# Hybrid decoder layer on one core: loads, closings, pacing and the weighting of the carried keys are changed

## The chip, the cores and the metric

The kernel runs on one core of a Trainium2 chip. The core has five engines: TensorE (PE in the profile; its weight loads are PEld), VectorE (DVE), ScalarE (ACT), GpSimd (POOL) and SyncE (SP), which here issues the DMA transfers. The metric is the device time of one execution in microseconds; lower is better. Kernels are compared by the medians of several executions.

## The reference

One decoder layer on x of 1024 tokens x 1024 features in fp32, with a memory of 256 tokens:

```
h   = rmsnorm(x, ln1);  z = h @ w_in            # mLSTM q,k,v,o,gates; forgetting q,k,v,gates
ml  = mlstm_chunkwise(silu(conv(q)), silu(conv(k)) * dh**-0.5, v, i, log_sigmoid(f))   # 4 heads of 128
        # carried along:  C = decay*C + sum_s wa_s v_s k_s ;  n = decay*n + sum_s wa_s k_s
        # num = scores @ v + inter * C q ;  den = sum(scores) + inter * n.q ;  out = num / max(|den|, exp(-m))
fx  = softmax(q k^T * dh**-0.5 + c_t - c_s, causal) @ v      # 8 heads of 64, c = cumsum(log_sigmoid(f))
x  += concat(norm(ml) * sigmoid(o), fx) @ w_out
x  += cross_attention(rmsnorm(x, ln_x), rmsnorm(mem, ln_mem))  # 4 heads of 256
x  += relu(rmsnorm(x, ln2) @ w_ff1)**2 @ w_ff2               # 1024 -> 4096 -> 1024
out = rmsnorm(x, ln_f)
```

## The kernel before

**Numbers.** A product in fp32 is made of three matmuls with operands split in a high and a low half (`mm3`, L184: low x high, high x low, high x high; these are L186, L187 and L188 in the profile). `split` (L131) makes the halves: ScalarE copies the high half (L134, or L137 with a scale), VectorE subtracts to get the low one (L135, or L138).

**Tiles.** Working tiles come from tagged slots: `w2` is 128x512 with a letter (`r_a` to `r_y` in the profile), `z` tiles are 128x1024 and a little more, `w` and `act` are larger. A tile waits until the tile that had its slot before is done with. PSUM has banks of 128x512 with tags `mm`, `m2` (or `m`), `tp`, `sc`, `ov`. Weights come into `wr` (two tiles of 128x1024) and are cut into `wh` and `wl` (three each).

**What sets the order.** The Python code issues the instructions in a program order; a scheduler with a simulated time then orders them on each engine, by what it takes to be ready first. Only inside `in_order` (L144), which the forgetting stage uses for each slot, does an engine keep the order of the code. All transfers go through SP's queue, in the order there; a transfer whose tile is not free holds those behind it.

**Stages.** First come norms, memory, values and gates; then the four mLSTM heads with the projections of the next head and of the forgetting heads' queries and keys (to about 365 us of the profiled execution); the forgetting heads' scores and values, beside them the filler (to about 605); the rest of the out projection (`w_out_b`), cross-attention and its out projection (to about 860); the MLP's first product, called Up here (to about 1200); its second, Down.

**mLSTM.** Time is cut in two halves of 512. `ml_project` (L657) makes a head's activated keys: `conv_silu` (L500) multiplies, convolves and ends with VectorE's L513 (y = (tanh + 1) * y, feature-major, 128 features x 1024 tokens). `fx_project` does a forgetting projection in between, and then `carried` (L517) makes the state that the first half leaves to the second: it loads the row's maximum, ScalarE makes four columns of weights from the gates (L522), TensorE transposes the first half of the keys (L527), VectorE multiplies the transposed keys by the weights (L529) and the result is split (L536). TensorE then forms the matrix (L540) and, with four matmuls against a column of ones (L542), the vector n_. `carry` (L554) uses both. `ml_head` (L569) does the scores of a head in a generator, whose closing part is stepped through by the next head's `ml_project`.

**Forgetting heads.** `slot` (L1026) does one step of several pipelines at once: transposes of one block of probabilities (`Values.turn`, L779), the product of an earlier one (`add`, L798), maxima (L741, L744), the split of the transposed block (`cut`), ScalarE's exponential (L756, into probabilities, from the bank of `sc` that a `score` of an earlier slot filled), GpSimd's scaling (L760), the next `score` (L728; matmuls L734, L735). When a half of a head has had its last product, `fx_close` (L805) copies the upper half of its `ov` bank with ScalarE (L810) and VectorE adds the lower (L811); the slot after that does no product. `sc` has three uses in flight at most, so a score waits for the exponential of an earlier part.

The filler (L1007) is work that the attention does not need: `key_unit`, `value_unit` (cross-attention's keys and values from the memory) and 16 `out_unit`s (out projection of the part that is there already, weights `w_out_a`). Each is a generator of steps of three matmuls, and each step says what it costs: 1.5 for keys and values, 3.0 for out. A slot n takes steps until the sum of the costs has reached (n − 3) x 4.6 (`RATE`, `DELAY`) or a unit ends. `cut_next` cuts at most one or two half weight tiles per slot (ScalarE L988; VectorE and GpSimd L989) once they are three slots old, and then the next load is issued. What is left of the filler runs behind the last slot without a slot's order (L1108).

**Up.** The product with `w_ff1` is done in blocks of 2 x 2 with seven products instead of eight. `todo` has 16 pairs of weight tiles; `left_up` (L1242) loads a pair (`raw_pair`, L1232: SP, tiles `wr` for odd pairs, two `z` tiles for even ones) and makes the left operands in three groups: group 0 splits the first tile and the half x22 of the second, and forms the sums x21 + x22 (L1256), and from it three further ones (L1257 to L1260; `sub` is L1223), on GpSimd for pairs 2 to 15. `prepare` calls it five jobs ahead of the first job that needs the group; a job is one of the seven products, 12 matmuls. VectorE and GpSimd also form sums of the results, and SP stores them (`put_right`, L1426).

## Time and profile before

| | |
|---|---|
| median of 3 executions | 1522.53 us (1520.9 to 1523.7) |
| profiled execution | 1523.35 us, span of its instructions 1521.6 us |
| mean granted TensorE clock | 0.998 |
| TensorE busy | 1502.7 us, 99% of the span |
| VectorE, ScalarE, GpSimd busy | 1100.3, 727.7, 510.1 us |
| DMA | 299.86 MB, 197 GB/s on the mean |

The profiled execution is 0.8 us above the median. In the profile, a row of a timeline has the start, the length, the engine, the line, the operation, what it writes and reads, shapes, and in brackets how long the engine stood idle before it and what ended the wait. The chain that ended last goes over TensorE for 93% of the span.

### The profile page before, as it was taken

To read this page: it belongs to the slowest core of one execution; us is meant where nothing else is said; L and a number is where in the kernel's file an instruction comes from. 1 tells how busy PE (TensorE), PEld (TensorE's weight loads), DVE (VectorE), ACT (ScalarE), POOL (GpSimd) and SP (SyncE) were. 2 spreads that over 40 slices of the span, in tenths; PEclk is the share of its full clock that TensorE was granted. 3 is DMA by queue.
4 is the path that set the end of the run, shared out by engine and by line. 5 is a ranking of instruction groups with operands and counts; after the bars stand their busy time and mean duration, and the time that the engine had idled before them with its cause. 6 is when DMAs were issued, how large, how long until landed. Compare 5 with 4: busy or idle time off the path is not lost.

```text
span 1521.6 us, 21977 instructions
## 1 busy us (share of the span) xinstructions
PE 1502.7 (99%) x7694; PEld 1261.5 (83%) x7694; DVE 1100.3 (72%) x1743; ACT 727.7 (48%) x1360; POOL 510.1 (34%) x543
## 2 busy tenths in 40 slices
PE   9999999999999999999999999999999999999997
PEld 9988888889999788888888877778787888888887
DVE  7766676765787786944457989898887667787665
ACT  7324343334687665644443456666664621122124
POOL 1003030413364442511110034544555265663322
PEclk9999999999999999999999999999999999999999
DMA  6322223435888886843344437776678777776623
GB/s 239 109 77 87 98 100 114 135 126 157 246 244 267 260 264 230 300 131 124 119 147 157 153 134 277 247 256 242 222 252 286 291 277 276 276 270 248 239 94 111
DMA packets 122538, 299.86 MB, mean 197 GB/s; under 512 B 13614, under 2 KB 28264, under 8 KB 115516
## 3 DMA queue, kind: packets, MB, share of 16 engines
q1 hardware_dynamic: 122428, 298.46, 57.4%
q8 instruction: 60, 0.98, 0.3%
q14 instruction: 50, 0.41, 0.1%
HBM read 199.60 MB, written 98.81 MB: 196 GB/s over the span
## 4 chain that ended last, share of the span: by engine, by line
PE 93%; DVE 3%; ACT 2%; DMA 1%; issue 1%; SPq 0%; DVEq 0%; POOLq 0%; POOL 0%; ACTq 0%
PE tp L186 8%; PE tp L187 8%; PE tp L188 8%; PE m L186 6%; PE sc L186 6%; PE m L187 6%; PE m L188 6%; PE sc L187 6%; PE sc L188 6%; PE mm L186 6%; PE mm L187 6%; PE mm L188 6%; PE ov L186 2%; PE ov L187 2%; PE ov L188 2%; PE ov L801 2%
## 5 line engine op out<-in xcount | busy, mean ns | idle before, releaser
L186 PE MATMUL tp<-act,wl 128*128 128x512 f32 (+1 forms) x440 | 172.9, 393 | 1.2 <-ACT row L1396 0.7
L187 PE MATMUL tp<-act,wh 128*128 128x512 f32 (+1 forms) x440 | 172.1, 391 | 0.0
L188 PE MATMUL tp<-act,wh 128*128 128x512 f32 (+1 forms) x440 | 171.7, 391 | 0.0
L135 DVE TENSOR_TENSOR wl<-wr,wh 128x1024 fp32r<-128x1024 f32 (+2 forms) x95 | 124.5, 1311 | 22.0 <-ACT wh L134 21.4
L134 ACT ACTIVATE wh<-wr 128x1024 fp32r<-128x1024 f32 (+2 forms) x95 | 95.6, 1007 | 75.9 <-PE tp L188 34.7
L186 PE MATMUL mm<-act,wl 128*128 128x512 f32 (+1 forms) x332 | 127.5, 384 | 0.0
L188 PE MATMUL mm<-act,wh 128*128 128x512 f32 (+1 forms) x332 | 127.3, 383 | 0.0
L187 PE MATMUL mm<-act,wh 128*128 128x512 f32 (+1 forms) x332 | 127.2, 383 | 0.0
L186 PE MATMUL m<-act,wl 128*128 128x512 f32 (+1 forms) x308 | 117.7, 382 | 0.5 <-DVE wl L135 0.5
L188 PE MATMUL m<-act,wh 128*128 128x512 f32 (+1 forms) x308 | 117.7, 382 | 0.0
L187 PE MATMUL m<-act,wh 128*128 128x512 f32 (+1 forms) x308 | 117.5, 381 | 0.0
L186 PEld LDWEIGHTS tp<-act,wl 128*128 128x128 f32 x440 | 82.6, 188 | 20.6 <-ACT row L1396 1.2
L188 PEld LDWEIGHTS tp<-act,wh 128*128 128x128 f32 x440 | 82.6, 188 | 18.9
L187 PEld LDWEIGHTS tp<-act,wh 128*128 128x128 f32 x440 | 82.7, 188 | 18.5
L186 PE MATMUL sc<-act,wl 128*128 128x512 f32 (+1 forms) x248 | 97.0, 391 | 1.0 <-DVE wl L135 1.0
L188 PE MATMUL sc<-act,wh 128*128 128x512 f32 (+1 forms) x248 | 96.7, 390 | 0.0
L187 PE MATMUL sc<-act,wh 128*128 128x512 f32 (+1 forms) x248 | 96.6, 390 | 0.0
L1467 POOL TENSOR_TENSOR z<-wr 128x256 f32<-128x256 f32 x56 | 51.7, 944 | 130.6 <-DMA wr<-w_ff2q 116.8
L134 ACT ACTIVATE wh<-z 128x1024 fp32r<-128x1024 f32 (+1 forms) x54 | 55.5, 1028 | 80.8 <-POOL z L1467 58.4
L135 DVE TENSOR_TENSOR wl<-z,wh 128x1024 fp32r<-128x1024 f32 (+1 forms) x54 | 74.3, 1376 | 7.8 <-ACT wh L134 7.6
L134 ACT ACTIVATE w<-wr 128x768 fp32r<-128x768 f32 (+2 forms) x31 | 25.5, 823 | 106.2 <-PE tp L186 33.7
L188 PEld LDWEIGHTS mm<-act,wh 128*128 128x128 f32 x332 | 62.3, 188 | 12.7
(726 smaller groups left out, 4288.4 us busy)
## 6 DMA issues: line engine op xcount, KB each, us to landing
act<-right SPq DMA_DIRECT2D x49, 1024.0 KB
right<-w SPq DMA_DIRECT2D x56, 256.0 KB
wr<-w_ff2q SPq DMA_DIRECT2D x28, 512.0 KB
right<-r_d SPq DMA_DIRECT2D x49, 256.0 KB
right<-r_e SPq DMA_DIRECT2D x49, 256.0 KB
act<-fqk SPq DMA_DIRECT2D x48, 256.0 KB
wr<-w_in SPq DMA_DIRECT2D x20, 512.0 KB
wr<-w_ff SPq DMA_DIRECT2D x20, 512.0 KB
```

The costliest lines, as they stand in the source:

```text
L134: s.activation(hi, src, AF.Copy)
L135: return v.tensor_tensor(out=lo, in0=src, in1=hi.bitcast(F32), op=ALU.subtract)
L186: nc.tensor.matmul(ps, w[1], x[0], start=first, stop=False, skip_group_check=more)
L187: nc.tensor.matmul(ps, w[0], x[1], start=False, stop=False, skip_group_check=more)
L188: nc.tensor.matmul(ps, w[0], x[0], start=False, stop=last, skip_group_check=more)
L801: nc.tensor.matmul(self.ov[:, c0:], self.fv[:, self.j], t[:, c0:], start=self.j == 0 and t is self.p[1], stop=self.last and t is self.p[0])
L1467: g.tensor_tensor(out=o, in0=x, in1=y, op=op)
```

## The change

It has four parts.

1. *mLSTM.* The gates also store `rels`, the first half of the rows `rel`, to DRAM. A new function `weigh`, called ahead of the keys' projection, loads the maximum and the head's row of `rels` broadcast over 128 partitions, into a `w2("b")` tile, and ScalarE takes the exponential of 128x512 there. `carried` then multiplies the keys by this row and sums over the columns in one VectorE instruction (n_ comes from its accumulator), before the transposes. TensorE transposes the weighted keys, the split is taken from PSUM, and the four matmuls against ones are gone.
2. *Forgetting, closings.* The loop with `fx_close` moves behind the exponentials and the scaling in `slot`.
3. *Forgetting, pacing.* Steps of key and value units count as 1.8, those of out units as 2.6.
4. *Up.* From pair 2 on, `raw_pair` loads the pair's second tile first, into the first of the two slots.

```diff
--- before.py
+++ after.py
@@ -446,6 +446,7 @@
     rows = dram.tile([MLH, T], F32, name="rows")
     gcol = const("gcol", [P, 8, MLH])
     emc = const("emc", [P, 8, MLH])
+    rels = dram.tile([MLH, TH], F32, name="rels")
     decay = dram.tile([2, 2, GW, T], F32, name="decay")
 
     def gate_rows():
@@ -469,6 +470,7 @@
         neg = on
         v.tensor_scalar(out=neg[0:MLH], in0=run[0:MLH], scalar1=-1.0, scalar2=None, op0=ALU.mult)
         load(rows, neg[0:MLH])
+        load(rels, rel[0:MLH, :TH])
 
     def gate_cols():
         for dst, src in ((gcol, rel), (emc, steps)):
@@ -514,39 +516,36 @@
         split(hi, lo, y, 0.5)
         return y
 
-    def carried(hd, y):
+    def weigh(hd):
 
         cols = col("m", 8, 1)
-        m0, m1, n_, wc = (cols[:, i:j] for i, j in ((0, 1), (1, 2), (2, 3), (4, 8)))
-        load(m0, rows[hd : hd + 1, TH - 1 : TH].broadcast_to([P, 1]))
-        s.activation(wc, gcol[:, 0:4, hd], AF.Exp, bias=m0)
-        v.tensor_scalar(out=wc, in0=wc, scalar1=0.5 * float(P) ** -0.5, scalar2=None, op0=ALU.mult)
+        yw = w2("b")
+        load(cols[:, 0:1], rows[hd : hd + 1, TH - 1 : TH].broadcast_to([P, 1]))
+        load(yw, rels[hd : hd + 1].broadcast_to([P, TH]))
+        s.activation(yw, yw, AF.Exp, bias=cols[:, 0:1])
+        return cols, yw
+
+    def carried(hd, y, cols, yw):
+
+        m0, m1, n_ = (cols[:, i : i + 1] for i in range(3))
+        v.tensor_tensor_reduce(out=yw, in0=y[:, :TH], in1=yw, scale=0.5 * float(P) ** -0.5, scalar=0.0, op0=ALU.mult, op1=ALU.add, accum_out=n_)
         kt = mm() if hd else sc()
         turn[0] += hd == 0
         for j in range(4):
-            nc.tensor.transpose(kt[:, j * P : (j + 1) * P], y[:, j * P : (j + 1) * P], ident)
-        kw = w2("c")
-        v.tensor_tensor(
-            out=kw.rearrange("p (j c) -> p j c", j=4),
-            in0=kt.rearrange("p (j c) -> p j c", j=4),
-            in1=wc.rearrange("p (j o) -> p j o", o=1).broadcast_to([P, 4, P]),
-            op=ALU.mult,
-        )
+            nc.tensor.transpose(kt[:, j * P : (j + 1) * P], yw[:, j * P : (j + 1) * P], ident)
         kh, kl = w2("d", dt=F32R), w2("e", dt=F32R)
-        split(kh, kl, kw)
+        split(kh, kl, kt)
         ps = mm()
         for j in range(4):
             for t in (kl, kh):
                 nc.tensor.matmul(ps[:, 0:256], t[:, j * P : (j + 1) * P], mv_of(hd, j), start=j == 0 and t is kl, stop=j == 3 and t is kh)
-        for j in range(4):
-            nc.tensor.matmul(ps[:, 256:257], kw[:, j * P : (j + 1) * P], ones, start=j == 0, stop=j == 3, skip_group_check=True)
         c32 = w2("c", P)
         s.activation(c32, ps[:, P : 2 * P], AF.Copy)
         v.tensor_tensor(out=c32, in0=ps[:, 0:P], in1=c32, op=ALU.add)
         c2 = w2("p", 2 * P, F32R)
         hi, lo = c2[:, 0:P], c2[:, P:]
 
-        v.tensor_scalar(out=n_, in0=ps[:, 256:257], scalar1=0.5, scalar2=None, op0=ALU.mult)
+        v.tensor_scalar(out=n_, in0=n_, scalar1=0.5, scalar2=None, op0=ALU.mult)
         v.tensor_scalar(out=m1, in0=m0, scalar1=-1.0, scalar2=None, op0=ALU.mult)
         split(hi, lo, c32)
         return m1, (hi, lo), n_
@@ -657,11 +656,12 @@
     def ml_project(hd):
         qk = quarters(F32R) if hd % 2 else [w4(dt=F32R) for _ in range(4)]
         q, k = qk[:2], qk[2:]
+        weighed = weigh(hd)
         yk = conv_silu(MLH + hd, *k)
         next(closing, None)
         fx_project(0, hd)
         next(closing, None)
-        state = carried(hd, yk)
+        state = carried(hd, yk, *weighed)
         next(closing, None)
         yq = conv_silu(hd, *q)
         fx_project(1, hd)
@@ -878,7 +878,7 @@
             ps = mm()
             for k in range(KT):
                 mm3(ps[:, :NM], both(w, lambda t: t[:, k]), (hm[:, 0, k], hm[:, 1, k]), k == 0, k == KT - 1)
-                yield 1.5, k == KT - 1, lambda: sink(ps)
+                yield 1.8, k == KT - 1, lambda: sink(ps)
 
         def sink(ps):
             t = rotate(*ROOM).rearrange("p (e c) -> p e c", e=2)
@@ -900,7 +900,7 @@
                 for k in range(KT):
                     x = (hm[:, 0, k, t * P : (t + 1) * P], hm[:, 1, k, t * P : (t + 1) * P])
                     mm3(ps, x, both(ws[k // 4], lambda z: z[:, k % 4]), k == 0, k == KT - 1)
-                    yield 1.5, k == KT - 1, lambda: sink(t, ps)
+                    yield 1.8, k == KT - 1, lambda: sink(t, ps)
 
         def sink(t, ps):
             o = rotate(*ROOM).bitcast(F32R).rearrange("p (e c) -> p e c", e=2)
@@ -950,7 +950,7 @@
             ps = mm()
             for k in range(MLH + KX):
                 mm3(ps, both(w, lambda t: t[:, k]), mixes[hf][k], k == 0, k == MLH + KX - 1)
-                yield 3.0, k == MLH + KX - 1, lambda: sink(x, ps)
+                yield 2.6, k == MLH + KX - 1, lambda: sink(x, ps)
 
         def sink(x, ps):
             v.tensor_tensor(out=x, in0=ps, in1=x, op=ALU.add)
@@ -1047,10 +1047,6 @@
             if x:
                 x.cut()
                 adds.append(x)
-            for hd, hf, ov in ended:
-                fx_close(hd, hf, ov)
-                if hd % 2:
-                    stores.append((hd, hf, True))
             exps = topped[:]
             topped[:] = tops
             for t, e in exps:
@@ -1058,6 +1054,10 @@
             while exped:
                 exped.pop(0).scale()
             exped.extend(t for t, e in exps if e == len(t.parts) - 1)
+            for hd, hf, ov in ended:
+                fx_close(hd, hf, ov)
+                if hd % 2:
+                    stores.append((hd, hf, True))
             fx_step()
             mix_step()
             part = next(parts, None)
@@ -1231,9 +1231,11 @@
 
     def raw_pair(p_, n0, n1):
         raws = [sb("wr", [P, 1024], 2) if p_ % 2 else z4()[:, :1024] for _ in range(2)]
+        if p_ > 1:
+            n0, n1 = n1, n0
         for raw, n in zip(raws, (n0, n1)):
             load(raw, a["w_ff1"][n])
-        return raws
+        return raws[::-1] if p_ > 1 else raws
 
     todo = [(b, k, 4 * b + k, 4 * b + 2 + k) for b in range(NB) for k in range(2)]
 
```

What the change does to the order of instructions follows for the places that the prediction speaks of. A row has line, operation, tile written, tiles read, shape; the numbers behind the names count tiles and differ between the two kernels.

First, VectorE in the last mLSTM head, from the end of the keys to the split of the carried keys. `z_401` (after: `z_403`) are the keys, `r_p` belongs to the closing of the head before, `r_e` to its scores; before:

```order
L513 SCALAR_TENSOR_TENSOR z_401_2658<-z_398_2604,z_401_2658 128x1024
L135 TENSOR_TENSOR r_e_2562<-r_c_2557,r_d_2561 128x256
L138 SCALAR_TENSOR_TENSOR act_2597<-z_401_2658,act_2597 128x1024
L642 SCALAR_TENSOR_TENSOR r_p_2736<-m_410_2711,row 128x512
L135 TENSOR_TENSOR wl_2949<-wr_2946,wh_2948 128x1024
L600 TENSOR_TENSOR r_f_2353<-ov_2504,r_f_2353 128x512
L135 TENSOR_TENSOR r_p_2736<-r_p_2736,r_p_2738 128x512
L529 TENSOR_TENSOR r_c_2761<-tp_2756,c_m_2752 128x512
L135 TENSOR_TENSOR r_e_2764<-r_c_2761,r_d_2763 128x512
```

and after (the two rows of L531 are the weighting and the reading of its sum; `r_b_2589` is the row of weights):

```order
L515 SCALAR_TENSOR_TENSOR z_403_2653<-z_400_2599,z_403_2653 128x1024
L135 TENSOR_TENSOR r_p_2699<-r_p_2699,r_p_2701 128x512
L531 ISA r_b_2589,c_m_2588<-z_403_2653,r_b_2589 128x512
L531 ISA c_m_2588 128x1
L135 TENSOR_TENSOR r_e_2552<-r_c_2547,r_d_2551 128x256
L548 TENSOR_SCALAR c_m_2588<-c_m_2588 128x1
L138 SCALAR_TENSOR_TENSOR act_2587<-z_403_2653,act_2587 128x1024
L641 SCALAR_TENSOR_TENSOR r_p_2731<-m_412_2706,row 128x512
L135 TENSOR_TENSOR wl_2935<-wr_2932,wh_2934 128x1024
L135 TENSOR_TENSOR r_p_2731<-r_p_2731,r_p_2733 128x512
L599 TENSOR_TENSOR r_f_2343<-ov_2494,r_f_2343 128x512
L135 TENSOR_TENSOR r_e_2754<-tp_2748,r_d_2753 128x512
```

The multiplication by weights stood behind the transposes and eight other instructions; it now stands two behind the end of the keys, with one split of 128x512 between.

TensorE in the second head, where `m_209` is the carried state; before and after:

```order
L540 MATMUL m_209_1588<-act_106,r_e_1585 128x256
L540 MATMUL m_209_1588<-act_106,r_d_1584 128x256
L542 MATMUL m_209_1588<-ones,r_c_1582 128x1 x4
L187 MATMUL mm_1650<-act_105,wh_1618 128x512
L188 MATMUL mm_1650<-act_104,wh_1618 128x512
```

```order
L541 MATMUL m_209_1586<-act_106,r_e_1583 128x256
L541 MATMUL m_209_1586<-act_106,r_d_1582 128x256
L188 MATMUL mm_1644<-act_104,wh_1612 128x512
L186 MATMUL mm_1644<-act_104,wl_1613 128x512
L187 MATMUL mm_1644<-act_105,wh_1612 128x512
```

The four matmuls against `ones` are gone and projections follow the state's own matmuls directly.

Second, ScalarE around a slot of the forgetting stage that closes a half of a head (L810), before and after; `act` and `w` are probabilities, `wh` is a filler weight:

```order
L756 ACTIVATE w_670_4182,c_den_4287<-sc_4288,c_mx_4286 128x512
L134 ACTIVATE r_b_4323<-r_b_4323 128x256
L134 ACTIVATE w_719_4386<-tp_4378 128x512
L810 ACTIVATE r_c_4389<-ov_4196 64x512
L756 ACTIVATE act_4317,c_den_4319<-sc_4320,c_mx_4318 128x512
L988 ACTIVATE wh_4404<-wr_4291 128x512
L134 ACTIVATE r_d_4414<-tp_4408 128x512
L756 ACTIVATE act_4317,c_den_4319<-sc_4362,c_mx_4318 128x128
```

```order
L756 ACTIVATE w_670_4155,c_den_4255<-sc_4256,c_mx_4254 128x512
L988 ACTIVATE wh_4302<-wr_4162 128x512
L134 ACTIVATE w_716_4341<-tp_4333 128x512
L756 ACTIVATE act_4288,c_den_4290<-sc_4291,c_mx_4289 128x512
L810 ACTIVATE r_c_4347<-ov_4173 64x512
L134 ACTIVATE r_d_4379<-tp_4373 128x512
L756 ACTIVATE act_4288,c_den_4290<-sc_4325,c_mx_4289 128x128
```

The closing stood ahead of the exponential of its slot (`sc_4320`) and now stands behind it (`sc_4291`). TensorE in the two slots behind that exponential, before, and the slot that answers to the second of them, after:

```order
L734 MATMUL sc_4398<-act_3190 128x512
L735 MATMUL sc_4398<-act_3190 128x512
L782 MATMUL tp_4408<-ident,act_3921 128x128 x4
L734 MATMUL sc_4421<-act_3190 128x256
L735 MATMUL sc_4421<-act_3190 128x256
L782 MATMUL tp_4431<-ident,act_3921 128x128 x4
L801 MATMUL ov_4345<-r_e_4355,w_618_3927 128x512
L801 MATMUL ov_4345<-r_d_4354,w_618_3927 128x512
L801 MATMUL ov_4345<-w_719_4386,w_618_3927 128x512 x2
```

```order
L782 MATMUL tp_4373<-ident,act_3907 128x128 x4
L734 MATMUL sc_4386<-act_3176 128x256
L735 MATMUL sc_4386<-act_3176 128x256
L186 MATMUL mm_4360<-act_3819,wl_4240 128x256
L187 MATMUL mm_4360<-act_3819,wh_4239 128x256
L188 MATMUL mm_4360<-act_3819,wh_4239 128x256
```

Before, the slots had transposes, products and scores only; now a filler's matmuls (L186 to L188 into `mm`) follow the score.

Third, GpSimd in Up. `z_1817` and `z_1818` (left operands) are one pair's tiles, `z_1868` (after: `z_1867`) is the next even pair's second tile, `r_f` a difference of results; before and after:

```order
L1223 TENSOR_TENSOR z_1817_9950<-r_b_9958,z_1818_9951 128x512
L1260 TENSOR_TENSOR z_1817_9950<-z_1817_9950,r_c_9959 128x512
L1223 TENSOR_TENSOR r_f_10030<-w_1825_9985,r_f_10030 128x512
L1256 TENSOR_TENSOR z_1868_10291<-z_1868_10291 128x512
L1223 TENSOR_TENSOR wr_10121<-wr_10121,wr_10120 128x512
```

```order
L1223 TENSOR_TENSOR z_1818_9937<-r_b_9944,z_1817_9936 128x512
L1262 TENSOR_TENSOR z_1818_9937<-z_1818_9937,r_c_9945 128x512
L1258 TENSOR_TENSOR z_1867_10276<-z_1867_10276 128x512
L1223 TENSOR_TENSOR r_f_10016<-w_1825_9971,r_f_10016 128x512
L1223 TENSOR_TENSOR wr_10106<-wr_10106,wr_10107 128x512
```

The first sum of the next even pair (L1256, now L1258) stood behind the difference `r_f` and now stands ahead of it.

## Prediction

> **What bounds the kernel.** I read the page's first part, then a table by stage, then TensorE's waits in the stages where the table shows it idle, and the chain of work that ended last for the places of those waits. The first fence is a line of the page and the rows by stage; in those, the second number is the length, and then come the busy microseconds of PE (TensorE), PEld (weight loads), DVE (VectorE), ACT (ScalarE) and POOL (GpSimd), the granted clock, the DMA share and GB/s.
>
> ```profile
> PE 1502.7 (99%) x7694; PEld 1261.5 (83%) x7694; DVE 1100.3 (72%) x1743; ACT 727.7 (48%) x1360; POOL 510.1 (34%) x543
> ...
> 40.00:365.00 325.00, 325.00 (x1754) 277.36 (x1753) 211.87 (x342) 121.14 (x212) 63.63 (x78) 1.00 0.34 107
> 395.00:480.00 85.00, 82.00 (x598) 75.88 (x597) 69.22 (x190) 67.65 (x184) 46.12 (x65) 1.00 0.82 239
> 480.00:605.00 125.00, 122.82 (x687) 103.74 (x686) 92.17 (x230) 81.10 (x220) 48.79 (x85) 1.00 0.85 259
> 860.00:1200.00 340.00, 337.26 (x1445) 270.01 (x1444) 295.85 (x339) 215.38 (x338) 147.31 (x96) 1.00 0.68 240
> ```
>
> TensorE is busy in 1502.7 of 1521.6 us. From 40 to 365 us (values, gates, the mLSTM heads) it has no gap at all, so there only less work on TensorE can shorten the kernel. It loses 3.0 us from 395 to 480 and 2.2 us from 480 to 605 (the forgetting heads beside the filler), and 2.7 us from 860 to 1200 (Up). The rest of its idle time lies at the start and after 1480 us, where the change does nothing. What it waited for in the two stages, forgetting first (total, times, longest):
>
> ```profile
> PE sc L734 <- ACT w L756: 2.8, 5, 1.3
> PE sc L734 <- ACT act L756: 1.4, 2, 1.0
> ...
> PE sc L186 <- DVE wl L135: 1.0, 2, 0.5
> PE tp L186 <- ACT row L1396: 0.7, 1, 0.7
> PE tp L186 <- DVE wl L135: 0.5, 1, 0.5
> PE m L186 <- DVE wl L135: 0.5, 1, 0.5
> ```
>
> In the forgetting stage 2.8 + 1.4 = 4.2 of the 5.2 us lost are waits of the score matmul (L734) until ScalarE's exponential (L756) has emptied a bank of `sc`. In Up, four waits of 0.5 us each are for the low half of a weight tile (L135).
>
> **mLSTM: the work removed.** The four matmuls of L542 per head (the sum of the weighted keys) go. The chain has them as pieces; first and last of four:
>
> ```profile
> 98.82 0.79 PE tp L542 x8
> ...
> 305.91 0.79 PE mm L542 x8
> ```
>
> 4 heads x 0.79 = 3.2 us of TensorE in a stage without a gap: −3.2. The transposes stay (same shape and type). On VectorE the product from PSUM goes and a fused multiply-and-sum over 512 columns comes; ScalarE's exponential of 4 columns becomes one of 512. Neither engine limits this stage (212 and 121 of 325 us busy), so the cost is nothing as long as TensorE never waits for them. That depends on one place: the transposes used to need only the activated keys (L513), and now need the new product after them. Its price is that of the causal mask's fused pass (L744); it stands in place of L529:
>
> ```profile
> 389.23 0.76 DVE L744 CUSTOM_DVE_ANT_0 sc<-sc,causal,c_mx 128x512 f32<-128x512 f32 x1
> ...
> 299.49 0.69 DVE L529 TENSOR_TENSOR r_c<-tp,c_m 128x512 f32<-128x512 f32 x1
> ```
>
> 0.76 instead of 0.69 us, and not behind the transposes but ahead of them. (An accumulator read follows it, for which the transposes need not wait.) The room, in heads 2 and 4, is between the end of L513 and the start of the transposes L527:
>
> ```profile
> 151.52 1.21 DVE L513 SCALAR_TENSOR_TENSOR z<-z,z 128x1024 f32<-128x1024 f32 x1
> 152.65 0.96 DVE L135 TENSOR_TENSOR r_e<-r_c,r_d 128x256 fp32r<-128x256 f32 x1
> 155.16 0.60 PE L527 MATMUL tp<-ident,z 128*128 128x128 f32 x4
> ...
> 293.08 1.21 DVE L513 SCALAR_TENSOR_TENSOR z<-z,z 128x1024 f32<-128x1024 f32 x1
> 294.21 0.96 DVE L135 TENSOR_TENSOR r_e<-r_c,r_d 128x256 fp32r<-128x256 f32 x1
> 293.24 1.66 POOL L594 TENSOR_TENSOR r_b<-r_c,r_b 128x256 f32<-128x256 f32 x1 [1.30 <-DVE r_c L590]
> 295.78 0.60 PE L527 MATMUL tp<-ident,z 128*128 128x128 f32 x4
> ```
>
> Head 2: the keys end at 152.73; with the split of 0.96 that follows them, the product ends at about 154.5, before 155.16. Head 4: they end at 294.29, and in the new order a split of 128x512 follows (front, first order). The split that followed before took 0.96 for half of that size and ended only at 295.17, 0.27 after GpSimd's product (293.24 + 1.66 = 294.90). A whole split that can end about 0.6 after GpSimd's (the 0.69 of a 128x512 row, less a little) is done at 295.5, the product at 296.2, and TensorE, due at 295.78, waits 0.4. Head 1's transposes were moved behind more matmuls, and head 3's keep their place with more room. So I take −3.2 + 0.4 = −2.8. Bounds: no wait at all (−3.2); or the product exposed in all four heads, 4 x 0.76 = 3.0 (−0.2). The new load of the weights' row is issued where the first half's sums have just freed its buffer, a projection ahead of the transposes; on SP's queue it holds weight loads whose tiles are cut one projection later, which hides that. ScalarE's longer exponential (0.69 in L756's row at 430.07, below) falls into gaps of an engine that is busy for 121 of 325 us.
>
> A rule speaks against this term. The Trainium skill (SBUF — State Buffer, section Who interferes with whom) says that a VectorE instruction with two inputs in SBUF is held by a GpSimd instruction that reads SBUF, for the whole of it, while one with at most one SBUF input, outside the two-port modes, is not. The trace agrees at 294.21, where half a split takes 0.96 under GpSimd's product. The old multiplication read its keys from PSUM, the new one reads both inputs from SBUF, so by the rule one that fell wholly under such a GpSimd row would be held for up to 1.66 us, and with that in one head the term would be −1.1 instead of −2.8. I leave it out, since GpSimd is done at 294.90, before the new product's turn.
>
> **Forgetting: closings behind the exponentials, and pacing.** A closing copies a bank of `ov` on ScalarE (L810). Before, it stood ahead of the slot's exponential, and the score in the next slot waited for that. The two costliest places (ScalarE's rows, and TensorE's that waited):
>
> ```profile
> 429.45 0.59 ACT L810 ACTIVATE r_c<-ov 64x512 f32<-64x512 f32 x1
> 430.07 0.69 ACT L756 ACTIVATE act<-sc,c_mx 128x512 f32<-128x512 f32 x1
> 430.90 0.39 PE L734 MATMUL sc<-act 128*128 128x256 f32 x1 [1.03 <-ACT act L756]
> ...
> 503.13 0.47 ACT L988 ACTIVATE wh<-wr 128x320 fp32r<-128x320 f32 x1 [2.16 <-DMA wr<-w_out_a]
> 504.01 0.59 ACT L810 ACTIVATE r_c<-ov 64x512 f32<-64x512 f32 x1
> 504.63 0.37 ACT L756 ACTIVATE w<-sc,c_mx 128x128 f32<-128x128 f32 x1
> 505.14 0.50 PE L734 MATMUL sc<-act 128*128 128x512 f32 x1 [1.33 <-ACT w L756]
> ```
>
> At 429.45 the closing delays the exponential by 0.62 us (429.45 to 430.07). The slots there had no filler either: the front's second order shows two slots in a row in which TensorE had only transposes, products and scores. After the change the closing stands behind, and the slots have 4 and 3 filler steps, so all 1.03 us go. At 504.01 the closing is again 0.62, but ScalarE had first stood 2.16 us for a weight load of the filler (L988); 0.62 of the 1.33 goes. The other waits:
>
> ```profile
> 475.99 0.50 PE L734 MATMUL sc<-act 128*128 128x512 f32 x1 [0.49 <-ACT w L756]
> 479.27 0.39 PE L734 MATMUL sc<-act 128*128 128x256 f32 x1 [0.42 <-ACT w L756]
> 514.28 0.39 PE L734 MATMUL sc<-act 128*128 128x256 f32 x1 [0.34 <-ACT act L756]
> 531.61 0.50 PE L734 MATMUL sc<-act 128*128 128x512 f32 x1 [0.17 <-ACT w L756]
> ```
>
> 514.28 and 531.61 are closing slots (0.34 + 0.17, both go). 475.99 and 479.27 (0.49 + 0.42) follow the other pair of slots without filler. Counted in the order, slots without filler were numbers 7, 17, 18, 28, 38, 39 before, counting from 0 at the first slot with values, and are 7, 32, 45 now, each alone; the single ones of before (7 and 28) cost nothing, so these two waits go. Sum: 1.03 + 0.62 + 0.34 + 0.17 + 0.49 + 0.42 = 3.1 us gained. Behind the closing stand only the next slot's split and the `ov` bank, which nobody writes in the next slot (a slot after a last product skips its products). Against it: 16 output units now take 5 x 2.6 = 13.0 units of a budget of 4.6 per slot, 2.8 slots instead of 3.3, so their weight loads have less time, in a stretch where DMA is at 0.85. I allow one more short wait, +0.5: −2.6. Bounds: all 4.2 us of waits for exponentials go (−4.2); or nothing goes and two more places like 505.14 arise (+2.7). The pacing moves no work: the same number of filler steps is left behind the last slot with values in both orders.
>
> **Up: the second tile of a pair first.** For pairs 2 to 15 the first of two loads now brings the tile of rows 21/22, which GpSimd's first sum (L1256) needs alone. SP waits for the same buffers as before, so the loads are issued at the same times with their contents exchanged:
>
> ```profile
> 949.73 0.33 SPq L1235 DMA_DIRECT2D z<-w_ff  x1
> 954.23 0.33 SPq L1235 DMA_DIRECT2D z<-w_ff  x1
> 958.78 1.34 POOL L1256 TENSOR_TENSOR z<-z 128x512 f32<-128x512 f32 x1 [5.66 <-DMA z<-w_ff]
> 960.09 1.75 POOL L1223 TENSOR_TENSOR wr<-wr,wr 128x512 f32<-128x512 f32 x1
> 958.29 2.39 DVE L135 TENSOR_TENSOR w<-w,r_d 128x512 fp32r<-128x512 f32 x2
> 960.60 1.78 DVE L1223 TENSOR_TENSOR w<-w,r_p 128x512 f32<-128x512 f32 x1
> 964.97 0.50 PE L186 MATMUL sc<-act,wl 128*128 128x512 f32 x1 [0.49 <-DVE wl L135]
> ```
>
> GpSimd stood 5.66 us for the second load and then summed from 958.78 to 961.84, just when VectorE was working towards the low half that TensorE waited for: two splits took 2.39 us and a difference 1.78, where a row of 128x512 takes 0.69 undisturbed (299.49). With the tile 4.5 us earlier the first sum runs at about 954.3, where VectorE waits for TensorE anyway; VectorE then meets one GpSimd instruction instead of two, and the low half is done about 1 us earlier, more than the 0.49 that TensorE lost. This comes four times, so up to −2.0. But in two of three pairs the order puts the first sum ahead of the difference of the results (front, third order), which delays that by about 1 us and moves GpSimd's work to other places under VectorE. I take half: −1.0; bounds −2.0 and +1.0 (two more such waits). The first tile comes 4.5 us later, but it is prepared five jobs of 12 matmuls each ahead of its first matmul.
>
> **Sum.** −2.8 − 2.6 − 1.0 = −6.4 us on the profiled execution's own 1523.35 us (span 1521.6 and 1.75 around it): 1516.95. The runs' median, 1522.53, lies 0.8 lower, so 1516.1 by the runs. All best bounds together give 1523.35 − 9.4 = 1514.0, or 1513.1 by the runs; all worst give 1523.35 + 3.5.
>
> **Rivals.** (1) Only the removed matmuls count: forgetting and Up give back elsewhere what they gain there (each 0 ± 1). For it: five of the waits are under 0.5 us, and such waits move easily. Against it: the closing and the empty slots are visibly gone from the order. 1522.5 − 2.8 = 1519.7, 1518.5 to 1521.
> (2) A wait takes the place of the removed matmuls: the transposes stand for the product in all heads, because GpSimd's products hold it or the row of weights comes late; −2.8 becomes −0.4 and the other two terms stay: 1518.5. For it: head 4 has no room. Against it: 0.7 us of room in head 2 with its held split counted.
> (3) Slower: the filler's weight loads. Each output unit has 0.5 slot less for its load; if ScalarE stands for them as at 503.13, the exponentials behind it are late and TensorE loses 1.33 each time. For it: one such case stands in the trace, at a DMA share of 0.85. Against it: of the score's waits listed above only that one has such a load in its chain. The sign turns at 5 more such waits (6.4 / 1.33 = 4.8); with 8 of the 16 units it is 1516.1 + 10.6 = 1526.7.
> (4) The exchange of loads does nothing, since GpSimd's sum stands behind other waits: Up 0, 1517.1, inside my forecast.
>
> **Chances.** The forecast with (4), 1513 to 1518.4: 0.63. Rival 1: 0.17, rival 2: 0.09, rival 3 with other losses: 0.11. A change of 0.2% is 3.0 us, about what a measurement can tell from none; the lines are 1519.5 and 1525.6. Faster: the forecast, most of rival 2 and a little less than half of rival 1: 0.63 + 0.06 + 0.06 = 0.75. Same: the rest of these two and the milder half of 3, 0.16; slower 0.09. The range leaves out the best bounds' last microsecond and the worse half of rival 3: 1512.5 to 1522.5.
>
> **What would show it.** Right: in the mLSTM stage TensorE still without a gap and the stage about 3 us shorter; in forgetting its waits for L756 down from 4.2 to about 1.5; in Up the 0.5 us waits for L135 gone or halved. Wrong: TensorE waiting at the transposes of `yw` for VectorE; ScalarE's waits for `w_out_a` more and longer than at 503.13, with exponentials behind them; new waits in Up from GpSimd's work under VectorE's splits. What I have not priced is the scheduler's different order between 600 and 660 us, where TensorE had no gap.

## The result, and the profile after

The changed kernel takes 1514.86 us (median of 6 executions, 1513.88 to 1516.84) against 1522.57 us before (6 executions, 1520.9 to 1524.11): 7.7 us less, ratio 0.9951, 95% interval 0.9939 to 0.9964. Forecast were 1516.1 us and a range of 1512.5 to 1522.5. The span of the profiled execution went from 1521.6 to 1514.5 us.

The page's first line and the four stages of the prediction, now of the kernel after (columns as before; its stages lie some 3 to 4 us earlier, so the windows are not quite the same work):

```profile
PE 1496.3 (99%) x7662; PEld 1258.1 (83%) x7662; DVE 1099.9 (73%) x1743; ACT 727.1 (48%) x1360; POOL 511.8 (34%) x543
...
40.00:365.00 325.00, 324.88 (x1748) 277.13 (x1748) 211.88 (x349) 124.06 (x215) 62.15 (x78) 1.00 0.36 112
395.00:480.00 85.00, 82.43 (x607) 77.54 (x607) 70.93 (x197) 69.04 (x188) 46.88 (x69) 1.00 0.84 239
480.00:605.00 125.00, 123.05 (x683) 104.29 (x682) 89.42 (x220) 77.28 (x208) 50.18 (x80) 1.00 0.80 256
860.00:1200.00 340.00, 339.27 (x1460) 273.01 (x1459) 296.16 (x337) 215.61 (x338) 151.19 (x100) 1.00 0.69 243
```

TensorE's idle time in Up has gone from 2.7 to 0.7 us; in the two forgetting windows it is 2.6 and 1.9 us where it was 3.0 and 2.2. The waits by what they waited for, first forgetting, then Up (total, times, longest):

```profile
PE sc L734 <- ACT act L756: 2.1, 1, 2.1
PE mm L187 <- DMA z<-mix: 2.0, 1, 2.0
PE tp L782 <- DVE r_b L138: 0.9, 1, 0.9
PE sc L734 <- ACT w L756: 0.5, 1, 0.5
...
PE tp L186 <- ACT row L1398: 0.7, 1, 0.7
```

In Up only the one wait for `row` is left that before had too. In forgetting the seven waits for exponentials have become two, of 2.1 and 0.5 us, and the wait for `mix` has grown from 0.3 to 2.0.

To see where the time went, the starts of four kinds of rows in the timelines divide every kernel's span: the first score of the forgetting stage (L734), the first transposes of cross-attention (L1185), the first squared result of Up (L1372), the end. Lengths in us, with the experiments told below (one profiled execution each):

| kernel | start to score | score to cross | cross to Up's square | to the end |
|---|---|---|---|---|
| before | 355.2 | 309.8 | 215.3 | 641.3 |
| changed | 352.0 | 309.0 | 215.3 | 638.2 |
| mLSTM part alone | 351.7 | 309.8 | 215.3 | 641.6 |
| closings alone | 355.0 | 306.9 | 215.3 | 640.9 |
| pacing alone | 355.3 | 314.1 | 215.3 | 641.8 |
| closings and pacing | 355.0 | 305.9 | 215.3 | 641.6 |
| Up alone | 355.2 | 307.7 | 215.3 | 638.4 |
| Up, even pairs | 355.2 | 309.2 | 215.3 | 640.0 |
| Up, odd pairs | 355.5 | 308.0 | 215.3 | 639.5 |
| changed, old pacing | 351.5 | 307.7 | 215.3 | 638.6 |
| changed, closings ahead | 352.5 | 311.5 | 215.3 | 638.1 |
| changed, out units 3.0 | 351.1 | 308.5 | 215.3 | 638.1 |
| changed, key and value units 1.5 | 351.1 | 310.9 | 215.3 | 638.1 |
| changed, `mix` earlier | 352.0 | 313.0 | 215.3 | 638.6 |

The first column falls into two groups, without the mLSTM part (mean of seven 355.2) and with it (mean of seven 351.7): 3.5 us. So does the last: 641.4 (mean of five without the exchange of loads) and 638.3 (mean of seven with it): 3.1 us. The second column is another matter: five kernels run the same code there (before, mLSTM alone, the three of Up) and take 307.7 to 309.8 us. What a part does to the forgetting stage is therefore read from the runs, not from one profile. Two of the profiles (pacing alone, and `mix` earlier) also hold a stretch with a lower granted TensorE clock in the second column; it is shown where these kernels are told.

### The profile page after: what moved, and what is told of

The parts are those of the page before. It is cut to its first block, busy times and chain, and to the rows that moved or that the text cites. A ratio compares the mean times of both kernels' runs of the same rounds, so it can differ in the third digit from the quotient of the medians.

```text
span 1514.5 us, 21910 instructions
## 1 busy us (share of the span) xinstructions
PE 1496.3 (99%) x7662; PEld 1258.1 (83%) x7662; DVE 1099.9 (73%) x1743; ACT 727.1 (48%) x1360; POOL 511.8 (34%) x543
## 4 chain that ended last, share of the span: by engine, by line
PE 88%; DMA 6%; DVE 3%; issue 1%; ACT 1%; SPq 0%; POOL 0%; DVEq 0%; POOLq 0%; ACTq 0%
PE tp L186 8%; PE tp L187 8%; PE tp L188 8%; PE sc L186 6%; PE sc L188 6%; PE sc L187 6%; PE m L187 5%; PE m L188 5%; PE m L186 5%; PE mm L187 5%; PE mm L186 5%; PE mm L188 5%; PE ov L186 2%; PE ov L187 2%; PE ov L188 2%; PE ov L801 2%
## 5 line engine op out<-in xcount | busy, mean ns | idle before, releaser
L186 PE MATMUL tp<-act,wl 128*128 128x512 f32 (+1 forms) x440 | 172.6, 392 | 0.7 <-ACT row L1398 0.7
L188 PE MATMUL tp<-act,wh 128*128 128x512 f32 (+1 forms) x440 | 171.7, 391 | 0.0
L188 PE MATMUL mm<-act,wh 128*128 128x512 f32 (+1 forms) x332 | 127.4, 384 | 0.0
L186 PE MATMUL mm<-act,wl 128*128 128x512 f32 (+1 forms) x332 | 127.3, 383 | 0.0
L188 PE MATMUL m<-act,wh 128*128 128x512 f32 (+1 forms) x308 | 117.6, 382 | 0.0
L186 PE MATMUL m<-act,wl 128*128 128x512 f32 (+1 forms) x308 | 117.5, 381 | 0.0
L186 PEld LDWEIGHTS tp<-act,wl 128*128 128x128 f32 x440 | 82.7, 188 | 19.7 <-ACT row L1398 1.2
L188 PEld LDWEIGHTS tp<-act,wh 128*128 128x128 f32 x440 | 82.7, 188 | 19.0
L188 PE MATMUL sc<-act,wh 128*128 128x512 f32 (+1 forms) x248 | 96.7, 390 | 0.0
L186 PE MATMUL sc<-act,wl 128*128 128x512 f32 (+1 forms) x248 | 96.6, 390 | 0.0
L135 DVE TENSOR_TENSOR wl<-z,wh 128x1024 fp32r<-128x1024 f32 (+1 forms) x54 | 78.5, 1454 | 10.4 <-ACT wh L134 10.3
L188 PEld LDWEIGHTS mm<-act,wh 128*128 128x128 f32 x332 | 62.3, 188 | 12.7
```

Source lines behind the costliest of these rows:

```text
L135: return v.tensor_tensor(out=lo, in0=src, in1=hi.bitcast(F32), op=ALU.subtract)
L186: nc.tensor.matmul(ps, w[1], x[0], start=first, stop=False, skip_group_check=more)
L188: nc.tensor.matmul(ps, w[0], x[0], start=False, stop=last, skip_group_check=more)
```

## The experiments

All ratios are to the kernel before, run in the same rounds. Line numbers of a kernel with the Up part are 2 higher from there on.

### Each part alone

The mLSTM part alone is the diff's hunks on `rels`, `weigh`, `carried` and `ml_project`:

```diff
+        load(rels, rel[0:MLH, :TH])
...
+        v.tensor_tensor_reduce(out=yw, in0=y[:, :TH], in1=yw, ..., accum_out=n_)
...
-            nc.tensor.matmul(ps[:, 256:257], kw[:, j * P : (j + 1) * P], ones, ...)
```

> The kernel before with the mLSTM part alone. Theory A (each part acts in its own stage): 3.3 us faster than before, all of it ahead of the first value transposes of the forgetting stage, no gap of TensorE from 40 us to there, the weighting (0.68 us in the changed kernel) not held by GpSimd; the later stages as before. Rival (a shift of 3 us changes what loads meet later): the stage gains 3.3 us but the total is more than 1 us off -3.3, with waits in forgetting or Up that before does not have.

Measured: 1520.0 us against 1522.65, ratio 0.9986 (0.9977 to 0.9994), so 2.1 us by the ratio (0.9 to 3.5); in the table 3.5 us ahead of the first score, no wait of TensorE between 40 us and there, and the later columns as before. The profile is theory A's, whose 3.3 us lie within the runs' interval too. In the forgetting stage one wait stands at another place than before: that of 1.33 us at 505.14 is absent, and there is one of 1.21 us, also behind a cut that stood for a weight load of the filler:

```profile
489.85 0.47 ACT L988 ACTIVATE wh<-wr 128x320 fp32r<-128x320 f32 x1 [3.15 <-DMA wr<-w_out_a]
491.32 0.50 PE L734 MATMUL sc<-act 128*128 128x512 f32 x1 [1.21 <-ACT act L756]
```

The closings alone (`fx_close` behind the exponentials, pacing 1.5 and 3.0):

```diff
-            for hd, hf, ov in ended:
-                fx_close(hd, hf, ov)
...
             exped.extend(t for t, e in exps if e == len(t.parts) - 1)
+            for hd, hf, ov in ended:
+                fx_close(hd, hf, ov)
```

> The kernel before with the closings behind the exponentials, old pacing. Theory A (the closing delays the exponential by 0.62 us and the score behind it by as much): the waits for L756 at the four closing slots (1.03, 1.33, 0.34, 0.17 us before) fall by 0.62 or to nothing, the two behind the other slots without filler (0.49, 0.42) stay; 1.7 to 2.5 us faster. Rival (the slots without filler make the score wait, closing or not): the waits move into the same slots behind the next exponential and the time stays within 0.7 us of before.

Measured: 1520.24 us, ratio 0.9984 (0.9975 to 0.9993), 2.4 us faster. The waits for L756 fell to 0.8 us in all; those at 475.99 and 479.27 went too, which theory A had kept. In place of some come waits that nobody had named, behind the closing itself; TensorE's rows of this kernel:

```profile
431.20 0.50 PE L801 MATMUL ov<-r_e,w 128*128 128x512 f32 x1 [0.40 <-DVE r_f L811]
476.87 0.50 PE L801 MATMUL ov<-r_e,w 128*128 128x512 f32 x1 [0.60 <-DVE r_f L811]
```

The product L801 takes up the bank that the closing's addition (L811) still reads. Both lie in the two places where two slots without filler follow each other.

The pacing alone:

```diff
-                yield 1.5, k == KT - 1, lambda: sink(ps)        # keys, and values alike
+                yield 1.8, k == KT - 1, lambda: sink(ps)
...
-                yield 3.0, k == MLH + KX - 1, lambda: sink(x, ps)
+                yield 2.6, k == MLH + KX - 1, lambda: sink(x, ps)
```

> The kernel before with the new pacing alone (1.8 and 2.6), closings ahead of the exponentials as before. Theory A (the pacing takes the slots without filler away, but moves the weight and mix loads into a busier stretch): the waits of 0.49 and 0.42 us go and that of 1.03 falls, but a wait of about 2 us behind a load of w_xv and about 1.6 us more for a load of mix come, as in the changed kernel; between 0 and 2 us slower. Rival (the pacing is the gain of this stage, the two long waits come from something else): 1 to 2.5 us faster without the two long waits.

Measured: 1523.67 us against 1522.65, ratio 1.0005 (0.9996 to 1.0014): no gain by itself. The wait for `mix` is 2.6 us in its profile; the waits for L756 are more in number (ten for seven) and little less in sum (3.7 us for 4.2). Behind `w_xv` there was only one of 0.6 us. This profile is of the slowest of its eleven executions, 1528.25 us, so its row in the table is no typical one. Behind the wait for `mix`, which ends at 513.92, the granted clock (third number from the end) is down for some 3 us:

```profile
515.00:516.00 1.00, 1.00 (x4) 0.86 (x3) 0.00 (x0) 0.06 (x1) 0.00 (x0) 0.50 0.86 323
518.00:519.00 1.00, 1.00 (x7) 0.80 (x6) 1.00 (x3) 0.00 (x0) 1.00 (x2) 1.00 0.02 6
```

Closings and pacing together, without mLSTM and Up (the last two diffs):

> The kernel before with both parts of the forgetting stage (closings behind, new pacing), nothing else. Theory A (parts add by stage: the changed kernel less mLSTM and Up is worth 1.8 us): 1.0 to 2.5 us faster than before, with waits of about 2 us for loads of w_xv or mix in place of the waits for exponentials. Rival (the two long load waits are made by the 3 us that the mLSTM part moves this stage): over 3 us faster, without a load wait above 1 us.

Measured: 1519.55 us against 1522.28, ratio 0.9982 (0.9973 to 0.9991): 2.7 us faster (1.4 to 4.1). Of TensorE's waits for L756 three are left, of 0.16 to 0.42 us, and no wait behind `w_xv`; the one for `mix` is there:

```profile
507.74 0.50 PE L187 MATMUL mm<-z,wh 128*128 128x512 f32 x1 [1.35 <-DMA z<-mix]
```

Neither expectation is met as it stands: the sum lies between theory A's (at most 2.5) and the rival's (over 3), and of the two long load waits only that for `mix` comes with these parts by themselves.

The exchange of loads alone:

```diff
+        if p_ > 1:
+            n0, n1 = n1, n0
...
-        return raws
+        return raws[::-1] if p_ > 1 else raws
```

> The kernel before with the second tile of a pair loaded first, nothing else. Theory A (GpSimd's sums under VectorE's splits made four low halves late): 2.5 us faster, all between the first and the last square of Up, the four waits of 0.5 us for L135 gone. Rival (the shift of the earlier stages, not the order of the loads, took the four waits away): under 0.7 us, waits of 0.5 us still there.

Measured: 1518.45 us, ratio 0.9977 (0.9968 to 0.9985), 3.5 us by the ratio, and 3.1 us in the table's last column. The four waits are gone. In this kernel's timeline the place that answers to the prediction's 958.78 reads (GpSimd, then VectorE):

```profile
950.48 2.04 POOL L1258 TENSOR_TENSOR z<-z 128x512 f32<-128x512 f32 x1 [0.20 <-DMA z<-w_ff]
956.06 1.67 POOL L1223 TENSOR_TENSOR wr<-wr,wr 128x512 f32<-128x512 f32 x1 [3.54 <-DVE r_c L135]
...
955.90 2.39 DVE L135 TENSOR_TENSOR w<-w,r_d 128x512 fp32r<-128x512 f32 x2
958.21 0.68 DVE L1223 TENSOR_TENSOR w<-w,r_p 128x512 f32<-128x512 f32 x1
```

GpSimd's first sum (L1258) stands 5.6 us ahead of the next one instead of directly ahead. The pair of splits is held as before (2.39 us), by the difference at 956.06; but VectorE's own difference behind it takes 0.68 us where it took 1.78. That is 1.1 us, as forecast.

### Which pairs

Even pairs lie in `z` tiles, odd ones in `wr` tiles. Each kind alone:

```diff
-        if p_ > 1:
+        if p_ > 1 and p_ % 2 == 0:        # the other kernel: == 1
             n0, n1 = n1, n0
```

> The kernel before with the exchange of the two loads for even pairs (z tiles) alone. Theory A (the four late low halves come from even pairs, where GpSimd stood 5.7 us for the second load and then summed beside VectorE's difference): all of the gain, 2.5 to 3.5 us, the four waits of 0.5 us gone. Rival (any earlier second tile shortens GpSimd's chain): half of it, 1.2 to 1.8 us.

> The same exchange for odd pairs (wr tiles) alone. Theory A: within 0.7 us of before, the four waits of 0.5 us still there. Rival: 1.2 to 1.8 us faster.

Measured: even pairs 1521.02 us against 1523.13, ratio 0.9988 (0.9979 to 0.9997); odd pairs 1520.37, ratio 0.9982 (0.9973 to 0.9991). The waits left for a low half, in Up, with even pairs exchanged and with odd ones:

```profile
1023.48 0.50 PE L186 MATMUL m<-act,wl 128*128 128x512 f32 x1 [0.52 <-DVE wl L135]
1141.88 0.50 PE L186 MATMUL sc<-act,wl 128*128 128x512 f32 x1 [0.51 <-DVE wl L135]
```

```profile
963.33 0.50 PE L186 MATMUL sc<-act,wl 128*128 128x512 f32 x1 [0.49 <-DVE wl L135]
1081.89 0.50 PE L186 MATMUL tp<-act,wl 128*128 128x512 f32 x1 [0.51 <-DVE wl L135]
```

Two of the four belong to each kind, and the table's last column loses about 1.5 and 1.9 us; by the runs it is 1.8 and 2.7 us. Theory A, that the even pairs cause all four, is wrong; the rival's halves are right.

### The parts of forgetting inside the changed kernel

Old pacing in the changed kernel, then the closings ahead of the exponentials again (the diffs above, reversed):

> The changed kernel with the old pacing (1.5 and 3.0). Theory A (the new pacing loses, here as alone, where it took 1.0 us more): 1 to 2 us faster than the changed kernel, so 1513 to 1514 us, without the waits of 2.1 us behind w_xv and 2.0 us for mix. Rival (the closings behind the exponentials need the new pacing, which fills the empty slots): 1515.5 to 1517 us, with the waits of 0.4 to 0.5 us behind slots without filler.

> The changed kernel with the closings ahead of the exponentials again, new pacing. Theory A (closings behind are worth 2.4 us, as alone): 1516.5 to 1517.5 us, with waits for L756 at the slots that close a half. Rival (with the slots filled, a closing no longer delays a score): within 0.7 us of the changed kernel.

Measured: with the old pacing 1515.24 us against 1523.13, ratio 0.9952 (0.9939 to 0.9964), not to be told from the changed kernel; with the closings ahead 1519.15, ratio 0.9976 (0.9967 to 0.9985), 3.8 us more by the two ratios, where the closings alone were worth 2.4. Part of the 3.8 may be the clock: four of the eleven executions with the closings ahead had a mean granted clock of 0.996, the others 0.997 or 0.998, and these four are the slowest (1520.75 to 1522.96); the median of the other seven is 1518.54, which still leaves some 3 us. So the closings carry this stage and the pacing adds nothing that these runs can show. Theory A's gain of 1 to 2 us from the old pacing did not come: the waits behind the closings (0.40 and 0.59 us for L811) were back, as the rival said, and the one for `mix` shrank only to 0.71.

Half of the pacing each: out units at 3.0 again, then key and value units at 1.5 again.

```diff
-                yield 2.6, k == MLH + KX - 1, lambda: sink(x, ps)
+                yield 3.0, k == MLH + KX - 1, lambda: sink(x, ps)
```

> The changed kernel with out units at 3.0 again, key and value units at 1.8. Theory A (1.8 moves the out units later and their loads against the last heads' loads; 2.6 makes the out units run faster than their weights come): without 2.6 less of the waits for w_out_a, the wait for mix stays at 1 us or more; within 1.5 us of the changed kernel either way. Rival (2.6 has to go with 1.8, since otherwise filler is left over behind the last slot): 1.5 us or more slower than the changed kernel.

```diff
-                yield 1.8, k == KT - 1, lambda: sink(ps)        # keys, and values alike
+                yield 1.5, k == KT - 1, lambda: sink(ps)
```

> The changed kernel with key and value units at 1.5 again, out units at 2.6. Theory A (1.8 is what fills the empty slots and what makes the load waits): the waits of 0.4 to 0.6 us behind the closings come back as with the old pacing, the wait for mix is under 1 us; within 1 us of the changed kernel. Rival (2.6 makes the load waits): a load wait above 1.5 us stays, 1.5 us or more slower than the changed kernel.

Measured: out units at 3.0 1514.82 us against 1522.28, ratio 0.9951 (0.9938 to 0.9963); key and value units at 1.5 1517.21, ratio 0.9965 (0.9953 to 0.9978), about 2.1 us more. The first keeps both long waits (1.56 us for L756 behind `w_xv`, 1.86 for `mix`), so these come with 1.8. The second has none for `mix`, but ScalarE waits for `w_out_a` five times (8.9 us), and TensorE 1.12 us behind one of them: 2.6 without 1.8 has the out units outrun their loads. For the first, theory A holds in the time and in the wait for `mix`, but ScalarE's wait for `w_out_a` is not less (4.6 us, in the changed kernel 3.8); for the second the rival does in its time, though the load's wait on TensorE is 1.1 and not 1.5 us, and the waits behind the closings that theory A named are back as well (0.40, 0.59 and 0.34 us).

### The wait for `mix`

The two long waits of the changed kernel, seen on ScalarE, TensorE and SP's queue:

```profile
446.39 1.42 SPq L975 DMA_DIRECT2D wr<-w_xv  x1
498.81 0.32 SPq L934 DMA_DIRECT2D z<-mix  x1
...
455.60 0.63 ACT L988 ACTIVATE wh<-wr 128x512 fp32r<-128x512 f32 x1 [2.82 <-DMA wr<-w_xv]
456.62 0.47 ACT L756 ACTIVATE act<-sc,c_mx 128x256 f32<-128x256 f32 x1
457.23 0.50 PE L734 MATMUL sc<-act 128*128 128x512 f32 x1 [2.06 <-ACT act L756]
507.32 0.51 PE L187 MATMUL mm<-z,wh 128*128 128x512 f32 x1 [1.95 <-DMA z<-mix]
```

The load of `w_xv` issued at 446.39 is waited for until 455.60, and the exponential and TensorE's score stand behind ScalarE's cut; the load of `mix` issued at 498.81 is waited for until 507.32. The last kernel starts the loads of `mix` two units of the filler earlier:

```diff
-            if u == len(units) - 2 * KT - 3:
+            if u == len(units) - 2 * KT - 5:
                 mix_in(0)
```

> The changed kernel with the loads of the first half of mix started two filler units earlier (15 places earlier on SP's queue). Theory A (the wait of 1.95 us for mix is a late load, a price of the new pacing): that wait goes, 1 to 2 us faster than the changed kernel, 1513 to 1514 us. Rival (DMA is full in this stretch, and an earlier load of mix makes weight loads late instead): the wait moves to L756 behind w_xv or w_xk, within 0.7 us of the changed kernel or slower.

Measured: 1519.54 us against 1522.28, ratio 0.998 (0.9972 to 0.9989), 4.4 us slower than the changed kernel by the ratios. The wait for `mix` is gone, and TensorE's waits behind ScalarE are these:

```profile
456.93 0.50 PE L734 MATMUL sc<-act 128*128 128x512 f32 x1 [2.11 <-ACT act L756]
486.77 0.80 PE L734 MATMUL sc<-act 128*128 128x512 f32 x1 [4.08 <-ACT act L756]
...
ACT wh L988 <- DMA wr<-w_xv: 7.1, 2, 4.2
```

The second is new: 4.1 us, again behind a load of `w_xv`. The rival is right: the earlier loads took the place of a weight's. But the waits are only part of the loss. All waits of TensorE in the table's second column add up to 5.8 us in the changed kernel and to 7.2 here, 1.4 more, while the column is 4.0 us longer. The rest is the granted clock, the third number from the end in these rows, behind the wait that ends at 486.77:

```profile
481.00:482.00 1.00, 1.00 (x8) 0.78 (x6) 0.96 (x3) 0.00 (x0) 0.16 (x1) 1.00 1.05 377
487.00:488.00 1.00, 1.00 (x3) 0.82 (x4) 0.97 (x4) 1.00 (x5) 0.68 (x2) 0.50 0.46 166
492.00:493.00 1.00, 1.00 (x6) 1.00 (x5) 0.57 (x3) 0.92 (x4) 0.00 (x0) 0.54 0.56 202
493.00:494.00 1.00, 1.00 (x12) 1.00 (x10) 0.43 (x2) 0.55 (x2) 0.88 (x2) 1.00 0.00 0
```

For about 6 us the clock is at half, and matmuls of 128x256 start 0.21 us apart there, where from 493 on it is 0.12; about 3 us of time, as an estimate from these rows. Behind the waits of 1.95 to 2.11 us in this profile and the changed kernel's the clock stays at 1.00; behind the 2.63 us of the kernel with pacing alone it fell. Nine of the eleven executions have a mean clock of 0.995 or 0.996, against 0.997 or 0.998 in all six of the changed kernel; but the other two, with 0.997, are no faster (1519.20 and 1519.39), so this division of the loss is shown for the profiled execution alone. No version here beats the changed kernel by more than the runs can tell.

## Why the prediction was right, and where it was not

**mLSTM (forecast −2.8).** The part is worth 3.5 us by the table's first column and 2.1 (0.9 to 3.5) by the runs. The step that failed is the wait of 0.4 us in head 4. After, VectorE, GpSimd and TensorE there:

```profile
289.04 1.21 DVE L515 SCALAR_TENSOR_TENSOR z<-z,z 128x1024 f32<-128x1024 f32 x1
290.17 1.23 DVE L135 TENSOR_TENSOR r_p<-r_p,r_p 128x512 fp32r<-128x512 f32 x1
291.32 0.68 DVE L531 CUSTOM_DVE_ANT_0 r_b<-z,r_b 128x512 f32<-128x512 f32 x1
289.20 1.65 POOL L593 TENSOR_TENSOR r_b<-r_c,r_b 128x256 f32<-128x256 f32 x1 [1.09 <-DVE r_c L589]
290.82 1.81 POOL L695 MEMSET act<- 64x2048 f32 x1
293.23 0.60 PE L535 MATMUL tp<-ident,r_b 128*128 128x128 f32 x4
```

The split of 128x512 was held as forecast (1.23 us, to 291.40, 0.55 after GpSimd's product ended at 290.85), and the product took 0.68. But the transposes start 2.98 us after the keys end (290.25), not 1.49 as before: TensorE, without a gap, has 1.5 us more of other work ahead of them. That they would still be due at 295.78 was the error. The new load and the longer exponential cost nothing, as said. By its 3.5 us the part also exceeds the bound of 3.2, the four pieces of 0.79. That term was sized by the chain's pieces and not from start to start. TensorE from the state's last matmul to the second projection behind it, in head 2 before and after:

```profile
164.78 0.28 PE L540 MATMUL m<-act,r_d 128*128 128x256 f32 x1
164.89 0.95 PE L542 MATMUL m<-ones,r_c 128*128 128x1 f32 x8
165.71 0.48 PE L187 MATMUL mm<-act,wh 128*128 128x512 f32 x1
166.03 0.39 PE L188 MATMUL mm<-act,wh 128*128 128x512 f32 x1
...
162.87 0.28 PE L541 MATMUL m<-act,r_d 128*128 128x256 f32 x1
162.99 0.40 PE L188 MATMUL mm<-act,wh 128*128 128x512 f32 x1
163.22 0.39 PE L186 MATMUL mm<-act,wl 128*128 128x512 f32 x1
```

The same two steps take 1.25 us with the matmuls against ones and 0.35 without, and it is so in all four heads (1.24 to 1.25, and 0.35 to 0.36). Each head saves 0.89, and four times that are 3.6 us: the 3.5 of the column. The runs' 2.1 is less, and their interval ends just below; what takes the rest there was not found.

The rule weighed there (Trainium skill, SBUF — State Buffer, section Who interferes with whom) did not reach the product: GpSimd's product had ended at 290.85. The same section of the Trainium skill says that a GpSimd instruction that only writes does not hold VectorE; these rows agree, since the product, with both inputs in SBUF, took 0.68 us inside GpSimd's memset of 290.82 to 292.63.

**Forgetting (forecast −2.6).** The two parts together measure −2.7 us (1.4 to 4.1), but by another sum, so that the size agrees is luck; in the table, one profile each, the stage is 3.9 us shorter with these parts alone and 0.8 in the changed kernel. Three steps were off. First, "0.62 of the 1.33 goes" rested on a wait that is no property of the code: the three kernels of Up run the same code in this stage, and their profiles have the other six waits, each within 0.1 us of its length, but none like that of 505.14; the mLSTM part alone, with this code too, has its wait behind a weight load at another score (1.21 us, shown above). Those of Up alone, to be held against 2.8 and 1.4 us before:

```profile
PE sc L734 <- ACT w L756: 1.6, 4, 0.5
PE sc L734 <- ACT act L756: 1.4, 2, 1.0
```

So 3.0 us in six waits where before had 4.2 in seven. In these five profiles of the same code, the wait behind a load of `w_out_a` comes, goes and moves, while the others stay. Second, the claim that nobody writes the closed `ov` bank in time was wrong with the old pacing (0.40 and 0.60 us in the kernel with closings alone). That is what the pacing is good for: without the double empty slots these waits do not arise, and it gives as much back in loads. Third, the allowance of 0.5 us for a later load was too small: `mix` took 2.0 and `w_xv` 2.1 us in the changed kernel's profile.

**Rival 3** is thus half true: late filler loads did take the place of the waits removed, twice and not eight times, and the loads were those of `w_xv` and `mix`, not of `w_out_a`. The wait behind `w_xv` stands in all three profiles that have the mLSTM part, the closings behind and key and value units at 1.8, and not in the one with closings and pacing alone, although SP's queue has the same order there. Why is open.

**Up (forecast −1.0).** It measures −3.1 us by the table and −3.5 (2.3 to 4.9) by the runs, beyond the best bound of −2.0. The mechanism was right, the step "I take half" was not: the new place of the first sum disturbed nothing, all four waits went. And a wait was sized by its bracket. Before, around the first of them (the row at 964.97 stands in the prediction, with 0.49 in brackets):

```profile
963.85 0.39 PE L187 MATMUL sc<-act,wh 128*128 128x512 f32 x1
964.08 0.40 PE L188 MATMUL sc<-act,wh 128*128 128x512 f32 x1
965.31 0.39 PE L187 MATMUL sc<-act,wh 128*128 128x512 f32 x1
```

Matmuls of this kind start 0.23 us apart, so the one at 964.97 was due at 964.31 and is 0.66 us late, since the bracket counts only from the end of the row ahead (0.40 long). The one behind it starts another 0.34 later instead of 0.23. From 964.08 to 965.31 are 1.23 us where two steps take 0.47: 0.76 lost, and 0.76 or 0.77 at the other three as well. Four times are the 3.1 us. In forgetting the same holds: the score at 430.90 follows transposes that start at 429.27 and last 0.60 in their row.

**Rivals 1 and 2** fell: both stages gain, and TensorE waits nowhere for the weighted keys. Rival 4 fell by 3.1 us. The forecast's total was 1.2 us short of the measured, mostly by Up. By the runs the three stages alone add up to 2.1 + 2.7 + 3.5 = 8.3 us, against 7.7 for all together; their intervals are too wide to call the 0.6 a loss.

## What to carry to other kernels

Size a wait on a pipelined engine by when the instruction was due, not by the idle time that its row shows, and price removed matmuls from start to start as well: here 0.77 for 0.49 us, and 0.89 for 0.79, four times each. Before a wait behind a DMA goes into a sum, look whether a second execution of the same code has it. When a late load is cured by an earlier one, look at the granted clock too, and not only at the waits. A buffer that several engines hand on has a due time as well: moving work behind one consumer (the closing behind the exponential) made the next writer of its bank wait, until the slots were filled.

## What the runs showed of the hardware that was not expected

With the loads of `mix` earlier, a wait of 2.0 us for them became one of 4.1 us for another load in a stretch where DMA is busy for some 80% of the time (0.84 and 0.80 in the windows above), and the granted clock was 0.50 for about 6 us behind it: the price of an earlier load was larger than that of the late one. And the same instructions of the forgetting stage took 307.7 to 309.8 us in five profiled executions, while the stage behind it took 215.3 us in all fourteen.
